# Weighted sums, row buffers and first lists in a hybrid decoder block with gathered experts

## The chip, the cores and the metric

The kernel runs on one core of one Trainium2 chip. The metric is the device time of one execution in microseconds; the time of a kernel is the median of several runs. The profile is one further execution, taken by the hardware profiler. Engines are named PE (TensorE matmul), PEld (TensorE weight load), DVE (VectorE), ACT (ScalarE), POOL (GpSimd) and SP (SyncE).

## The reference

A decoder block over 1024 tokens of width 1024, float32: three token mixers on one normalised input, gated and summed, and then a PEER mixer, in which each token picks 8 x 16 of 16384 experts. The diff is about the second half:

```python
def peer_ffn(h, w_q, subkeys, u, v):
    q = (hf @ w_q).reshape(T, PEER_HEADS, 2, PEER_HALF)
    sc = jnp.einsum('thpd,hpkd->thpk', q, subkeys)
    s1, i1 = lax.top_k(sc[:, :, 0], PEER_TOPK)
    s2, i2 = lax.top_k(sc[:, :, 1], PEER_TOPK)
    cand = (s1[..., :, None] + s2[..., None, :])      # 256 pairs a head
    top_s, pos = lax.top_k(cand, PEER_TOPK)
    ...
    gate = jax.nn.softmax(top_s, axis=-1)
    act = gelu(einsum('chkd,cd->chk', u[ic], hc))     # u rows of the picked experts
    w = gc * act
    return einsum('chk,chkd->cd', w, v[ic])           # weighted sum of their v rows
```

The mixers before it are stick-breaking attention (8 heads), a dilated window attention (12 heads in 3 groups) and cross-attention to 256 memory tokens, each with its own projection, `gates * y` summed, one output projection and the residual.

## The kernel before, in words

The 1024 tokens are 8 tiles of 128, in four groups of two (tiles 0 and 1, 2 and 3, 4 and 5, 6 and 7). `phase1` is a generator that takes one group through projections, the three mixers, gating, output projection, norm (`ffn_norm`), query products (`select`) and, as a side generator, the choice of experts (`topk`). `topk` of a tile makes 16 lists of 16 (`top16`, five VectorE calls each, for 8 heads x 2 halves) into `s16` and `i16`, combines them per head, and ends with the indices `iT` and gates `gT`.

The experts are then computed in one of two ways. Tiles 1, 3 and 5 (`DENSE`) go through all 16384 experts by plain matmul: `dense`, the last stage, streams both expert tables in 64 chunks. The other five tiles gather: 128 steps a tile (class `Experts`), in each of which one u row and one v row of 1024 are fetched per partition with an indirect DMA on POOL. A row here is such a pair of fetches for 128 partitions. In `step`, VectorE multiplies the u row with the token's own h (spread over partitions by a small matmul into `pb`) and sums it (L1037). Every fourth step closes a group of four rows, and a list `behind` runs its later parts one step at a time: `gelu`, then `weights` (the gates times the activations, spread to a 128 x 32 block `wz` per row), then `sums(0)` to `sums(3)`. A `sums` is four matmuls of 32 output columns over the v row, accumulated in `po` (L1061). `supply` fetches u rows ahead; v rows are fetched by `run_behind`, one step after their own.

The h used by the gathered tiles is written to DRAM by `ffn_norm` as three bf16 parts (`part`, L767 to L770, the write on ScalarE's queue) and read back per 32 tokens by `rows_of` into `b3`.

The order of the work: a loop at the end alternates `ex.step()` with `fill`, which advances `phase1` or `dense` by one step and then `nside` steps of the side list (one while rows are there, four while none are). Constants (`TOKEN_NS`, `BW`, `LEAST`) decide how much filling goes between two rows. A scheduler then orders the instructions of each engine from this source order and their readiness, and places waits; ScalarE alone keeps the order of the source.

Group 0 splits its weights and inputs into two float32r halves; the halves live in the row buffers (`spare`), since no rows are gathered yet. A weight is split two ahead of its use.

Of the kernel before, what the change touches and what calls it, by code (L numbers as in the profile page):

```python
# [39 lines left out]
LEAST = 3000.0  # L40
SPLIT = (0,)
AHEAD = 2
UP = 3
GMAX = max(GROUPS)
NMAX = GMAX * 128
QB = 8
# [27 lines left out]
def block_kernel(ctx: ExitStack, tc: tile.TileContext, io):  # L74
    nc = tc.nc
    pool = lambda name, bufs, **kw: ctx.enter_context(tc.tile_pool(name=name, bufs=bufs, **kw))
    gat = pool("gat", 3)
    gw = pool("gw", 2)
    sc = pool("sc", 2)
    keep = pool("keep", 4)  # L80
# [194 lines left out]
        nc.vector.tensor_sub(lo, src, hi)  # L275
        return hi, lo

    nspare = [0]

    def spare():  # L280

        nspare[0] += 1
        t = gat.tile([128, 2, D], F32, name="u" if nspare[0] % 2 else "v").bitcast(F32R)
        return t[:, 0], t[:, 1]

    class Weights:
        def __init__(self, gidx):
# [445 lines left out]
    def ffn_norm(x2, n0, G, h2T):  # L733
        gffn = wp.tile([128, 8, 128], F32, name="w").rearrange("p a b -> p (a b)")
        load(gffn, bass.AP(tensor=io["g_ffn"].tensor, offset=io["g_ffn"].offset,
                                        ap=[[0, 128], [1, D]]))
        h2s = []
        for i in range(G):
            h2 = big.tile([128, D], F32, name="big")
            st = small.tile([128, 4], F32, name="st")  # L740
            actf(h2, x2[:, i, :], AF.Square, accum_out=st[:, 0:1])
            actf(st[:, 1:2], st[:, 0:1], AF.Ln, scale=1.0 / D, bias=eps)
            actf(st[:, 1:2], st[:, 1:2], AF.Exp, scale=-0.5)
            actf(st[:, 2:3], st[:, 1:2], AF.Square)
            nc.vector.tensor_scalar(st[:, 3:4], st[:, 0:1], 1.0 / D, EPS, op0=OP.mult, op1=OP.add)
            nc.vector.scalar_tensor_tensor(st[:, 3:4], st[:, 2:3], -0.5, st[:, 3:4], op0=OP.mult, op1=OP.mult)
            nc.vector.scalar_tensor_tensor(st[:, 1:2], st[:, 3:4], 1.5, st[:, 1:2], op0=OP.add, op1=OP.mult)
            nc.vector.scalar_tensor_tensor(h2, x2[:, i, :], st[:, 1:2], gffn, op0=OP.mult, op1=OP.mult)
            nc.scalar.dma_start(xres[n0 + i], x2[:, i, :])
            h2s.append(h2)  # L750
            cost[0] += 1500
            yield
        for i, h2 in enumerate(h2s):
            for k in range(0, 8, 4):
                pt = bank()
                for j in range(4):
                    flip(pt[:, j * 128:(j + 1) * 128], h2[:, (k + j) * 128:(k + j + 1) * 128])
                actf(h2T[:, k:k + 4, i * 128:(i + 1) * 128], pt.rearrange("p (a b) -> p a b", a=4), AF.Copy)
            yield
        for i, h2 in enumerate(h2s):  # L760
            n = n0 + i
            if n in DENSE:
                nc.scalar.dma_start(h2d[DENSE.index(n)], h2T[:, :, i * 128:(i + 1) * 128])

            for part in range(3 if n not in DENSE else 0):
                b = gw.tile([128, D], BF, name="part", bufs=2)
                nc.vector.tensor_copy(b, h2)  # L767
                if part < 2:
                    nc.vector.tensor_sub(h2, h2, b)
                nc.scalar.dma_start(b3d[n, :, part], b)  # L770
                cost[0] += 1000
                yield
# [8 lines left out]
    def select(pipe, weights, h2T, n0, G, out):  # L781
        N = G * 128
        subk = big.tile([128, 16, 128], F32, name="big")
        load(subk, io["subk"])
        scs = [sc.tile([128, 16, 128], F32, name="sc") for i in range(G)]
        for hp in range(16):
            p = proj_T(weights("w_pq", hp), h2T, N)
            q = tmp.tile([128, NMAX], F32, name="q")
            actf(q[:, :N], p[:, :N], AF.Copy)

            def part(hp=hp, q=q):
                z = bank()
                for i in range(G):
                    mm(z[:, i * 128:(i + 1) * 128], q[:, i * 128:(i + 1) * 128], subk[:, hp, :],
                       start=True, stop=True)
                for i in range(G):
                    actf(scs[i][:, hp, :], z[:, i * 128:(i + 1) * 128], AF.Copy)
            pipe.tick()
            pipe.push(part)
            yield  # L800
        pipe.flush()
        side.append(topk(n0, G, scs, out))

    def topk(n0, G, scs, out):
        for i in range(G):
            s16 = tk.tile([128, 8, 2, 16], F32, name="s16")
            i16 = tk.tile([128, 8, 2, 16], U32, name="i16")  # L810
            for hp in range(16):
                top16(s16[:, hp // 2, hp % 2, :], i16[:, hp // 2, hp % 2, :], scs[i][:, hp, :])
                yield

            room = scs[i].rearrange("p a b -> p (a b)")
            cand = room[:, 0:896].rearrange("p (h c) -> p h c", h=8)
# [83 lines left out]
    def phase1(gidx, n0, G, out):  # L900
        N = G * 128
        pipe = Pipe()
        weights = Weights(gidx)
        xT = big.tile([128, 8, NMAX], F32, name="big")
        load(xT[:, :, :N], io["xT"][:, :, n0 * 128:n0 * 128 + N])
        hT = big.tile([128, 8, NMAX], F32, name="big")
        norm = norm_T(xT, N, g_mix, hT)
        if gidx == 0:
            memT = big.tile([128, 8, MEM], F32, name="big")
            load(memT, io["memT"])  # L910
            mh = big.tile([128, 8, MEM], F32, name="big")
            yield from norm_T(memT, MEM, g_mem, mh)
            kv = memory_kv(pipe, weights, both(gidx, mh, MEM))
            next(kv)
            next(norm)
            yield next(kv)
            next(norm)
            yield next(kv)
            hT = both(gidx, hT, N)
            yield from kv  # L920
            weights.ahead = AHEAD
            gap_tables()
        else:
            yield from norm
            hT = both(gidx, hT, N)
        oT = act.tile([128, 10, NMAX], F32, name="oT")
        yield from stick_breaking(pipe, weights, hT, n0, G, oT)
        mem = memory_attn(pipe, weights, hT, n0, G, oT)
        yield from dilated(pipe, weights, hT, n0, G, oT, mem)
        yield from mem  # L930
        mT = big.tile([128, 8, NMAX], F32, name="big")
        pipe.flush()
        yield from gating(pipe, weights, hT, N, oT, mT)
        x2 = big.tile([128, GMAX, D], F32, name="big")
        yield from out_proj(weights, mT, n0, G, x2)
        h2T = big.tile([128, 8, NMAX], F32, name="big")
        yield from ffn_norm(x2, n0, G, h2T)
        yield from select(pipe, weights, both(gidx, h2T, N), n0, G, out)


    def rows_of(n, c):
        b3 = gw.tile([96, D], BF, name="b3")
        nc.sync.dma_start(b3, b3d[n, c].rearrange("s t d -> (s t) d"))
        return b3

# [4 lines left out]
    class Experts:  # L950
# [5 lines left out]
        def __init__(self):  # L956
            self.tile = None
            self.us, self.vs = [], []
            self.todo = []
            self.behind = []  # L960
            self.late = []

        def fetch(self, kind, ap):

            q = self.us if kind == "u" else self.vs
            if kind not in self.__dict__ or self.__dict__[kind] is None:
                pair = gat.tile([128, 2, D], F32, name=kind)
                x = 0
                self.__dict__[kind] = pair
            else:  # L970
                pair, x = self.__dict__[kind], 1
                self.__dict__[kind] = None
            nc.gpsimd.indirect_dma_start(out=pair[:, x], out_offset=None, in_=io[kind],  # L973
                                         in_offset=bass.IndirectOffsetOnAxis(ap=ap, axis=0))
            q.append(pair[:, x])

        def supply(self):

            while len(self.us) < 2 * UP:
                if self.tile is None:  # L980
                    if not ready:
                        break
# [17 lines left out]
        def run_behind(self):  # L1000

            for it in list(self.behind):
                f = it.pop(0)
                if f:
                    f()
                if not it:
                    self.behind.remove(it)
            if self.late:
                self.fetch("v", self.late.pop(0))

        def step(self):

# [17 lines left out]
                    self.pbs.append(pb)  # L1030
                self.parts = gw.tile([128, 2, 4], F32, name="parts")
            self.run_behind()
            self.late.append(ap)
            u = self.us.pop(0)
            for hh, pb in enumerate(self.pbs):
                f = slice(hh * 512, (hh + 1) * 512)
# [2 lines left out]
            if i == 3:  # L1039
# [13 lines left out]
                def sums(i, wz=wz, box=box):  # L1053
# [10 lines left out]
                    if jj == QB - 1 and i == 3:  # L1064
                        row = box["row"]
                        nc.vector.tensor_add(row, row, po[:, h:h + 256])
                        for k, dst in enumerate(quarters(io["out"][n], c)):
                            nc.scalar.dma_start(dst, row[32 * k:32 * k + 32])
                first = lambda: (weights(), sums(0))
                self.behind.append([gelu, first] + [lambda x=x: sums(x) for x in (1, 2, 3)])  # L1070
            return g == 31 and i == 3

        def flush(self):
# [241 lines left out]
```

## Time and profile before

| | |
|---|---|
| median of 3 runs | 3846.92 us (3844.34 to 3854.73) |
| profiled execution | 3849.53 us |
| its span | 3847.7 us |
| mean granted TensorE clock | 0.964 |
| DMA moved | 1126.05 MB, mean 293 GB/s |
| PE busy | 3582.9 us (93%) |
| DVE busy | 2645.4 us (69%) |
| POOL busy | 1271.1 us (33%), 1280 of its instructions are the fetches |

How to read it: the span runs from the first to the last instruction. Shares of busy time are means over stages. Group 0 takes the first 517 us or so, without rows; groups 1 to 3 with rows beside them go to about 2480 us, the dense stage with the rows of tiles 6 and 7 from there to the end. The chain of waits is followed back from the last instruction; its shares say what set the end. Ends of matmuls are modelled, so matmul times are best read from start to start.

### The profile page before, as it was taken

Reading aid. Unit: us, or ns where it says so; the run is one execution under the profiler, and the core shown is the slowest. Engines: PE = TensorE matmul, PEld = TensorE weight load, DVE = VectorE, ACT = ScalarE, POOL = GpSimd, SP = SyncE. Lnnn points to the kernel's source line nnn. Section 1 sums busy time; section 2 is a strip of 40 time slices with the busy share of each in tenths; the row PEclk is TensorE's granted clock in tenths of the full one; section 3 lists DMA queues with packets and bytes.
Section 4 is the critical chain, followed back from the end, with each engine's and each line's share of the span. In section 5 each row is a group of like instructions: output and inputs, shape, how many; then the busy total and the mean of one; then the engine's idle time right before and its main releaser. Section 6 shows DMA issues by size and latency. Waiting matters only on the chain.

```text
span 3847.7 us, 63068 instructions
## 1 busy us (share of the span) xinstructions
PE 3582.9 (93%) x23493; PEld 2767.8 (72%) x23493; DVE 2645.4 (69%) x7899; ACT 1292.1 (34%) x2584; POOL 1271.1 (33%) x1288
## 2 busy tenths in 40 slices
PE   7999789899799999988999998689999999999999
PEld 6889766677576667767666677576777777777777
DVE  5443697555669656566965665498877877778776
ACT  3442443421225442123554312132322322222322
POOL 0000044333315434320553441024444444434442
PEclk9999899999899999989999999889999999999999
DMA  4435579799969989985998897478999999999995
GB/s 135 135 113 169 179 294 356 282 329 370 342 206 372 364 280 329 358 326 178 358 346 310 318 350 272 149 274 305 340 329 340 340 345 335 338 326 335 354 325 201
DMA packets 365950, 1126.05 MB, mean 293 GB/s; under 512 B 37196, under 2 KB 116812, under 8 KB 344908
## 3 DMA queue, kind: packets, MB, share of 16 engines
q0 software_dynamic: 184320, 671.17, 47.4%
q1 hardware_dynamic: 155024, 403.29, 30.0%
q10 hardware_dynamic: 26300, 47.55, 3.3%
q8 instruction: 186, 3.05, 0.3%
q14 instruction: 120, 0.98, 0.1%
HBM read 1072.78 MB, written 49.09 MB: 292 GB/s over the span
## 4 chain that ended last, share of the span: by engine, by line
PE 78%; DVE 11%; DMA 6%; ACT 2%; issue 1%; ACTq 0%; POOL 0%; SPq 0%; DVEq 0%; POOLq 0%
PE bank L112 36%; PE bank L1080 31%; PE po L1061 9%; DVE u L1037 2%; DMA w<-in_w_gate 2%; PE pb L1028 1%; DMA u<-in_u,iT 1%; DMA b3d<-part 1%; PE bank L116 1%; ACT e L123 1%; DVE ab L1099 1%; DVE sc L777 0%; DVE acc L1197 0%; DVE ab L1101 0%; DMA v<-in_v,iT 0%
## 5 line engine op out<-in xcount | busy, mean ns | idle before, releaser
L973 POOL DMA_INDIRECT u<-in_u,iT x640 | 641.9, 1003 | 1366.2 <-DVE i L776 508.8
L973 POOL DMA_INDIRECT v<-in_v,iT x640 | 628.3, 982 | 1169.9 <-PE po L1061 1041.2
L1037 DVE SCALAR_TENSOR_TENSOR u<-u,pb 128x512 f32<-128x512 f32 x1280 | 835.6, 681 | 69.5 <-DMA u<-in_u,iT 50.2
L112 PE MATMUL bank<-big,w 128*128 128x256 f32 x3072 | 725.1, 390 | 25.2 <-DMA w<-in_w_gate 13.7
L112 PEld LDWEIGHTS bank<-big,w 128*128 128x128 f32 x3072 | 581.5, 194 | 152.9 <-issue 49.0
L1061 PE MATMUL po<-v,wz 128*32 128x256 f32 x5120 | 425.9, 395 | 10.2 <-DVE wz L1050 9.2
L1080 PE MATMUL bank<-hh,uh 128*128 128x384 f32 x1024 | 350.2, 342 | 16.4 <-DVE pos L779 16.2
L1080 PE MATMUL bank<-hh,ul 128*128 128x384 f32 x1024 | 346.7, 339 | 5.2 <-DVE ul L1152 5.2
L1080 PE MATMUL bank<-hl,uh 128*128 128x384 f32 x1024 | 346.0, 338 | 0.0
L1197 DVE TENSOR_TENSOR acc<-acc,bank 128x512 f32<-128x512 f32 x384 | 258.7, 685 | 109.7 <-PE bank L1080 104.4
L1080 PE MATMUL bank<-vh,wh 128*128 128x512 f32 x768 | 324.1, 425 | 3.3 <-ACT wh L123 1.8
L1080 PE MATMUL bank<-vl,wh 128*128 128x512 f32 x768 | 300.2, 394 | 0.0
L1080 PE MATMUL bank<-vh,wl 128*128 128x512 f32 x768 | 298.6, 395 | 0.0
L112 PEld LDWEIGHTS bank<-w,big 128*128 128x128 f32 x2432 | 278.5, 192 | 21.7 <-issue 11.9
L112 PE MATMUL bank<-w,big 128*128 128x128 f32 x2432 | 288.8, 277 | 0.0
L123 ACT ACTIVATE big<-bank 128x128 f32<-128x128 f32 (+2 forms) x436 | 141.6, 419 | 404.2 <-PE bank L112 371.1
L123 ACT ACTIVATE vh<-vr 128x1024 fp32r<-128x1024 f32 x128 | 134.6, 1051 | 411.4 <-PE bank L1080 405.6
L1061 PEld LDWEIGHTS po<-v,wz 128*32 128x32 f32 x5120 | 116.6, 109 | 208.2 <-issue 136.4
L1080 PEld LDWEIGHTS bank<-vh,wh 128*128 128x128 f32 x768 | 143.8, 188 | 117.8 <-issue 70.0
L1080 PEld LDWEIGHTS bank<-hh,uh 128*128 128x128 f32 x1024 | 194.8, 190 | 32.9 <-issue 28.3
L1099 DVE TENSOR_SCALAR ab<-iota,sl 128x128 f32<-128x128 f32 x384 | 134.3, 350 | 104.7 <-PE bank L112 96.6
L1080 PEld LDWEIGHTS bank<-hh,ul 128*128 128x128 f32 x1024 | 195.0, 190 | 11.0 <-DVE ul L1152 9.0
(221 smaller groups left out, 5556.9 us busy)
## 6 DMA issues: line engine op xcount, KB each, us to landing
w<-in_w_in SPq DMA_DIRECT2D x136, 512.0 KB
ur<-in_uT SPq DMA_DIRECT2D x64, 1024.0 KB
vr<-in_vd SPq DMA_DIRECT2D x64, 1024.0 KB
w<-in_w_gate SPq DMA_DIRECT2D x96, 512.0 KB
w<-in_w_pq SPq DMA_DIRECT2D x64, 512.0 KB
gd<-big ACTq DMA_DIRECT2D x24, 1024.0 KB
g<-gd SPq DMA_DIRECT2D x32, 768.0 KB
w<-in_w_o SPq DMA_DIRECT2D x64, 256.0 KB
```

Of the source, the lines that this page charges most:

```text
L112: nc.tensor.matmul(out, lhsT, rhs, **kw)
L116: nc.tensor.transpose(out, in_, ident)
L123: nc.scalar.activation(out, in_, f, **kw)
L973: nc.gpsimd.indirect_dma_start(out=pair[:, x], out_offset=None, in_=io[kind], in_offset=bass.IndirectOffsetOnAxis(ap=ap, axis=0))
L1028: nc.tensor.matmul(pb, which[:, jj].rearrange("p q s -> p (q s)"), box["b3"][:, hh * 512:(hh + 1) * 512], start=True, stop=True)
L1037: nc.vector.scalar_tensor_tensor(u[:, f], u[:, f], 1.0, pb, op0=OP.mult, op1=OP.mult, accum_out=self.parts[:, hh, i:i + 1])
L1061: nc.tensor.matmul(po[32 * k:32 * k + 32, h:h + 256], wz[:, i, :], v[:, 256 * k:256 * k + 256], start=jj == 0 and i == 0, stop=jj == QB - ...
L1080: nc.tensor.matmul(out, lhsT, rhs, **kw)
L1099: nc.vector.tensor_scalar(ab[:, 0, :], iota, sl[:, 0, t:t + 1], sl[:, 2, t:t + 1], op0=OP.is_equal, op1=OP.mult)
L1197: nc.vector.tensor_add(acc[:, i, f], acc[:, i, f], o)
```

## The change

- The four sums of a group are issued together, one step after its weights, instead of one in each of four steps, the first with the weights.
- Rows have buffers of their own: five of u and seven of v, in place of three pairs each. u is fetched up to five ahead, v in the row's own step. `spare` takes one u and one v buffer.
- `part` and `b3` share one pool of three buffers (before: two each).
- `s16` and `i16` get a second buffer; the lists of a group's first tile are made inside `select`, one step behind the scores of each head half, and `topk` makes lists for the other tile alone.
- Group 0 does one more step of the memory projection before it splits hT.

```diff
-UP = 3
+UP, VP = 5, 7
...
-    gat = pool("gat", 3)
+    gat = pool("gat", 1)
...
+    def row_buffer(kind):
+        return gat.tile([128, D], F32, name=kind, bufs=UP if kind == "u" else VP)
     def spare():
-        nspare[0] += 1
-        t = gat.tile([128, 2, D], F32, name="u" if nspare[0] % 2 else "v").bitcast(F32R)
-        return t[:, 0], t[:, 1]
+        return row_buffer("u").bitcast(F32R), row_buffer("v").bitcast(F32R)
...
-                b = gw.tile([128, D], BF, name="part", bufs=2)
+                b = gw.tile([128, D], BF, name="b3", bufs=3)
...
+        s16 = tk.tile([128, 8, 2, 16], F32, name="s16", bufs=2)
+        i16 = tk.tile([128, 8, 2, 16], U32, name="i16", bufs=2)
...
+            def first(hp=hp):
+                top16(s16[:, hp // 2, hp % 2, :], i16[:, hp // 2, hp % 2, :], scs[0][:, hp, :])
             pipe.tick()
-            pipe.push(part)
+            pipe.push(part, first)
...
-            s16 = tk.tile([128, 8, 2, 16], F32, name="s16")
-            i16 = tk.tile([128, 8, 2, 16], U32, name="i16")
-            for hp in range(16):
-                top16(s16[:, hp // 2, hp % 2, :], i16[:, hp // 2, hp % 2, :], scs[i][:, hp, :])
-                yield
+            if i:
+                s16 = tk.tile([128, 8, 2, 16], F32, name="s16", bufs=2)
+                i16 = tk.tile([128, 8, 2, 16], U32, name="i16", bufs=2)
+                for hp in range(16):
+                    top16(s16[:, hp // 2, hp % 2, :], i16[:, hp // 2, hp % 2, :], scs[i][:, hp, :])
+                    yield
...
             yield next(kv)
+            yield next(kv)
             hT = both(gidx, hT, N)
...
-        b3 = gw.tile([96, D], BF, name="b3")
+        b3 = gw.tile([128, D], BF, name="b3", bufs=3)[:96]
...
-            while len(self.us) < 2 * UP:
+            while len(self.us) < UP:
...
-            if self.late:
-                self.fetch("v", self.late.pop(0))
...
-            self.late.append(ap)
+            self.fetch("v", ap)
...
-                first = lambda: (weights(), sums(0))
-                self.behind.append([gelu, first] + [lambda x=x: sums(x) for x in (1, 2, 3)])
+                self.behind.append([gelu, weights, lambda: [sums(x) for x in range(4)]])
```

More of the change, by code (lines that the diff above doesn't have):

```diff
@@ L276, in halves @@
         return hi, lo
-    nspare = [0]
+    def row_buffer(kind):
+        return gat.tile([128, D], F32, name=kind, bufs=UP if kind == "u" else VP)
     def spare():
-        nspare[0] += 1
-        t = gat.tile([128, 2, D], F32, name="u" if nspare[0] % 2 else "v").bitcast(F32R)
-        return t[:, 0], t[:, 1]
+        return row_buffer("u").bitcast(F32R), row_buffer("v").bitcast(F32R)
     class Weights:
@@ L797, in part, with topk @@
                     actf(scs[i][:, hp, :], z[:, i * 128:(i + 1) * 128], AF.Copy)
+            def first(hp=hp):
+                top16(s16[:, hp // 2, hp % 2, :], i16[:, hp // 2, hp % 2, :], scs[0][:, hp, :])
             pipe.tick()
-            pipe.push(part)
+            pipe.push(part, first)
             yield
         pipe.flush()
-        side.append(topk(n0, G, scs, out))
-    def topk(n0, G, scs, out):
+        side.append(topk(n0, G, scs, out, s16, i16))
+    def topk(n0, G, scs, out, s16, i16):
         for i in range(G):
-            s16 = tk.tile([128, 8, 2, 16], F32, name="s16")
-            i16 = tk.tile([128, 8, 2, 16], U32, name="i16")
-            for hp in range(16):
-                top16(s16[:, hp // 2, hp % 2, :], i16[:, hp // 2, hp % 2, :], scs[i][:, hp, :])
-                yield
+            if i:
[4 more added lines that the diff above has]
+                    yield
             room = scs[i].rearrange("p a b -> p (a b)")
@@ L960, in __init__ @@
             self.behind = []
-            self.late = []
         def fetch(self, kind, ap):
[L965 to L973, printed above, removed]
+            t = row_buffer(kind)
+            nc.gpsimd.indirect_dma_start(out=t, out_offset=None, in_=io[kind],
                                          in_offset=bass.IndirectOffsetOnAxis(ap=ap, axis=0))
-            q.append(pair[:, x])
+            (self.us if kind == "u" else self.vs).append(t)
         def supply(self):
-            while len(self.us) < 2 * UP:
+            while len(self.us) < UP:
                 if self.tile is None:
```

## The prediction

> **What bounds the kernel now.** I read the page's totals and its chain first, then the chain by stage, then busy times by stage.
>
> ```profile
> span 3847.7 us, 63068 instructions
> PE 3582.9 (93%) x23493; PEld 2767.8 (72%) x23493; DVE 2645.4 (69%) x7899; ACT 1292.1 (34%) x2584; POOL 1271.1 (33%) x1288
> PE 78%; DVE 11%; DMA 6%; ACT 2%; issue 1%; ACTq 0%; POOL 0%; SPq 0%; DVEq 0%; POOLq 0%
> ...
> by line: PE bank L112 59.8%; PE po L1061 10.2%; DVE u L1037 3.1%; DMA w<-in_w_gate 2.8%; DMA v<-in_v,iT 2.1%; PE bank L116 2.0%; issue 1.8%; DMA u<-in_u,iT 1.7%; PE pb L1028 1.2%; DVE ab L1099 1.2%; DMA b3d<-part 1.2%; DVE ab L1101 1.0%; DV
> by line: PE bank L1080 79.9%; PE po L1061 11.5%; PE pb L1028 2.0%; DMA u<-in_u,iT 1.8%; issue 1.1%; DVE u L1037 0.7%; POOL u L973 0.5%; DVE ul L1152 0.4%; DVE vl L1152 0.3%; DVE acc L1197 0.3%; ACTq L1068 0.2%; POOL v L973 0.2%; DVE w L1179
> ...
> 517.00:2480.00 1963.00, 1817.53 (x12377) 1353.15 (x12376) 1274.06 (x4648) 689.15 (x1579) 728.29 (x762) 0.96 0.86 313
> 2640.00:3848.00 1208.00, 1201.97 (x6992) 910.74 (x6991) 947.45 (x1963) 351.61 (x527) 494.00 (x474) 1.00 0.90 327
> ```
>
> The two "by line" rows are the chain from 1060 to 1740 us (a token group with the gathered rows beside it) and from 2640 to 3848 us (dense experts beside the rows). The window rows have length, then busy time of PE, PEld, DVE, ACT, POOL, then granted clock, DMA share, GB/s. TensorE is the bound: in the dense stage it is busy 1202 of 1208 us and holds 79.9 + 11.5 + 2.0 = 93% of the chain; in a group 59.8 + 10.2 + 2.0 + 1.2 = 73%. The weighted sums (po) alone are a tenth of the chain, so what they cost TensorE is what to price first.
>
> **One: four sums in one go.** A row's sum is four 32-column matmuls, eight records.
>
> ```profile
> L1061 PE MATMUL po<-v,wz x5120: 379/379/637, 526.1 to 3819.6; 128*32 128x256 f32 x197
> ...
> 2909.11 0.40 PE L1080 MATMUL bank<-vh,wl 128*128 128x512 f32 x1
> 2909.43 0.64 PE L1061 MATMUL po<-v,wz 128*32 128x256 f32 x8
> 2910.00 0.50 PE L1080 MATMUL bank<-vh,wh 128*128 128x512 f32 x1
> 2910.34 0.39 PE L1080 MATMUL bank<-vl,wh 128*128 128x512 f32 x1
> 2910.57 0.40 PE L1080 MATMUL bank<-vh,wl 128*128 128x512 f32 x1
> ...
> 3817.75 0.40 PE L1080 MATMUL bank<-vh,wl 128*128 128x512 f32 x1
> 3818.08 1.93 PE L1061 MATMUL po<-v,wz 128*32 128x256 f32 x32
> 3819.94 0.50 PE L1080 MATMUL bank<-vh,wl 128*128 128x512 f32 x1
> 3820.28 0.39 PE L1080 MATMUL bank<-vh,wh 128*128 128x512 f32 x1
> ```
>
> Undisturbed, 512-column matmuls start 0.23 us apart (2910.34 to 2910.57). A row alone costs 2910.34 - 2909.11 = 1.23 us less two such steps, 0.77. Four rows that happen to stand together (the flush at the end) cost 3820.28 - 3817.75 = 2.53 less 0.46, 2.07, where four alone cost 3.08. So each run of sums that is joined to its neighbour saves 1.01/3 = 0.335 us: 0.14 within the run, the rest at its borders, where the next matmuls start late. Counted in the timeline of TensorE from the first sum (526.1) to the last (3819.4), the 640 rows stand in about 560 runs: some 488 alone, 66 pairs, 4 threes, 2 fours. The source after the change makes 160 runs of four. 400 borders x 0.335 = 134 us of TensorE's time.
>
> Of the 1280 POOL fetches 474, 37%, fall into 2640 to 3848 us; with the dense stage's start I take 40% of the rows: 54 us, times the 93% that TensorE has of the chain, 50 us. The groups' 60%, 80 us, times 73% would be 59; right after each group's query products DVE is the fuller engine and in the gating stage weights are waited for (the w_gate entry, 2.8%), so I take 45, with 25 to 59 as ends. Sum: **-95 us**. The weights wz are made one step before the sums rather than in the same step, which takes away this wait of TensorE; I take 5 of it:
>
> ```profile
> PE po L1061 <- DVE wz L1050: 9.2, 8, 2.2
> POOL v L973 <- PE po L1061: 1041.2, 233, 37.2
> DVE u L1037 <- DMA u<-in_u,iT: 50.2, 37, 5.6
> u<-in_u,iT POOLq DMA_INDIRECT x640, 8.2
> ```
>
> **Two: single row buffers.** As many fetches, as many bytes, the same POOL work. The v fetch goes out in the row's own step, ahead of the next u fetch, instead of one step later. A v row of the last place in its group is asked for when the sums four steps before it have freed a buffer and is used four steps on, as now; the other three have more. POOL's 1041 us of waiting for po change shape, and POOL has nothing else to do, so that gains nothing. u is the risk: six rows in three pairs become five. Pace in the dense stage is 1208 us for 474/2 rows, 5.1 us a row, so five rows are 25.5 us ahead of use; a fetch lands after 8.2 us (last column of its row), and a wait for v ahead of it takes 1041.2/233 = 4.5. 12.8 us are left, so the mean fetch stays hidden; the late ones (50.2 us of DVE's waits now) get more by one row's time. I charge **+8**, ends 0 and 25 (half of today's 50 again).
>
> The spare halves in group 0 fall from six to five pairs. Five are enough when two hold h and three hold weights; the split of a weight is then freed by the projection before it, whose copy ScalarE waits for in its queue anyway. **+2**, ends 0 and 8. The added step before hT is split has the remaining memory projections as cover.
>
> **Three: one pool for part and b3.** Today the third bf16 part waits until the first has been written out, and ScalarE's queue, which issues that write, holds the query products behind it.
>
> ```profile
> 404.95 1.23 DVE L769 TENSOR_TENSOR big<-big,part 128x1024 f32<-128x1024 f32 x1
> 414.71 0.69 DVE L767 CAST part<-big 128x1024 bf16<-128x1024 f32 x1 [8.54 <-DMA b3d<-part]
> 418.08 0.80 PE L1080 MATMUL bank<-u 128*128 128x256 f32 x2 [12.94 <-ACT u L123]
> 1723.05 0.71 PE L112 MATMUL bank<-big,q 128*128 128x128 f32 x4 [2.03 <-ACT q L123]
> 2422.55 1.44 PE L1028 MATMUL pb<-b,which 96*128 96x512 bf16 x3 [12.29 <-DMA b<-b3d]
> 400.00:440.00 40.00, 25.77 (x185) 24.73 (x186) 21.94 (x50) 15.12 (x31) 0.00 (x0) 0.73 0.61 200
> ```
>
> With three buffers and no rows running (group 0), the third cast follows at 406.2, so 8.5 of the 12.9 us go. Group 2's last b3 is about done: 2. Group 1 still has a row tile in a buffer: 0. Group 3 makes six parts and then reads b3 into the same three buffers: the cast may come 6 us sooner, or the read 4 us later: 0. Together **-11**, ends -3 and -15. The clock in this window is 0.73; a hole of 4.4 us stays, and no row prices the clock for a hole that short, so I count nothing for it. [...]
>
> **Four: lists during the query products.** The source moves 16 calls of top16 (8 VectorE records each, no DMA) for each group's first tile. But the instruction order on VectorE is not the source's: the lists of the first tile stand among the query products already.
>
> ```profile
> 2435.03 0.29 DVE L775 MAX8 s<-sc 128x8 f32<-128x128 f32 x1 [2.09 <-ACT sc L123]
> 2436.56 0.28 DVE L779 FIND_INDEX8 i<-s,sc 128x8 uint32<-128x128 f32 x1
> 2438.93 0.29 DVE L775 MAX8 s<-sc 128x8 f32<-128x128 f32 x1 [2.09 <-ACT sc L123]
> 2420.00:2480.00 60.00, 57.45 (x279) 50.36 (x279) 24.07 (x113) 11.88 (x43) 0.00 (x0) 0.93 0.34 109
> 2500.00:2620.00 120.00, 96.79 (x544) 79.41 (x544) 117.35 (x374) 34.70 (x47) 36.03 (x32) 0.87 0.76 267
> ```
>
> One list takes 2435.03 to 2436.84 = 1.8 us and then waits 2.09 for the next scores. So the move itself is worth 0. What does change is that s16 and i16 get a second buffer: today the second tile's lists start only when the first tile has let go of them, in 2500 to 2620 us, where DVE is busy 117 of 120 us and TensorE misses 23. If they slip into the 2.09 us gaps, up to 16 x 1.8 = 29 us of DVE leave that stretch. I take half, **-15**, ends 0 (they stay) and -30. In group 0 the weight splits fill those gaps; nothing there.
>
> **Sum.** -95 - 5 + 8 + 2 - 11 - 15 = -116. The profiled execution took 3849.5 us (span 3847.7), 2.6 over the median of the runs shown: 3733 in its terms, **3731** in the median's.
>
> **Rivals.**
> - *The transfers become the bound.* DMA share is already 0.86 to 0.90 in the two long windows. For it: w_gate waits on the chain. Against it: 327 x 1208/1158 = 341 GB/s would do for the dense stage, and this window moved more:
> ```profile
> 1160.00:1220.00 60.00, 59.20 (x360) 39.57 (x360) 54.65 (x220) 31.77 (x50) 36.20 (x37) 1.00 0.99 379
> ```
>  Half of the 95 lost and 10 more of u waits: about 3789.
> - *The sums don't stay together.* Engine orders are not the source's, so a row whose v is thought late may be put behind other matmuls. Then parts two to four remain, -21 to -25: about 3825.
> - *Nothing measurable*: that, with part four worth nothing and u waits at their end: 3840 to 3855.
> - *Slower: the gather queue.* A v fetch at the head of POOL's queue now waits for a whole burst of sums, all u fetches behind it, with one u row less in store; a late u delays parts, wz, and TensorE's burst with all behind it. It decides once the 12.8 us reserve is gone and more than 116/160 = 0.73 us a group is lost; at 1 us a group 160 - 116 = +44, about 3893. The row of 1041 us speaks for it, the reserve against. [...]
>
> **How the numbers follow.** Forecast 0.66, transfers 0.14, sums apart 0.07, nothing 0.05, slower 0.08. The forecast's own ends: all the better ones (50 + 59 from the sums, 9 of wz, 15, 30) give about 3684, all the worse ones (50 + 25, nothing of wz, 3, nothing from part four, 33 lost) about 3802. The range 3690 to 3815 takes in the forecast and the transfers; left out are 0.20. Faster by over 0.3% (11.5 us, about what runs of this kernel can tell from nothing): 0.66 + 0.14 + 0.07 = 0.87; within 0.05; slower 0.08.
>
> **What will show it.** Right: po records in blocks of 32, 1.93 us each, about 160 runs; PE busy down by 100 us or more at a span down as much; the hole at 405 us down to some 4 us; lists of the second tile between 2425 and 2482. Wrong: po in eights; DVE's waits for u far over 50 us or TensorE's for v where there are none now; DMA share near 1.0 in the dense windows with TensorE no longer full.

## The result, and the profile after

| | before | after |
|---|---|---|
| median | 3850.77 us (3844.34 to 3854.73) | 3782.09 us (3779.82 to 3798.13) |
| span of the profiled execution | 3847.7 us | 3780.4 us |
| mean granted TensorE clock | 0.964 | 0.957 |
| PE busy | 3582.9 us | 3462.0 us |
| DMA moved | 1126.05 MB | 1126.09 MB |

The ratio is 0.9832, with a 95% interval of 0.98 to 0.9864: 69 us faster, where 116 were forecast. The page after: totals, the chain by engine, and the group of the sums (with that of before above it).

```profile
L1061 PE MATMUL po<-v,wz 128*32 128x256 f32 x5120 | 425.9, 395 | 10.2 <-DVE wz L1050 9.2 <-DMA v<-in_v,iT 0.8
```
```profile
span 3780.4 us, 63673 instructions
PE 3462.0 (92%) x23493; PEld 2829.0 (75%) x23493; DVE 2617.4 (69%) x7899; ACT 1297.7 (34%) x2588; POOL 1265.3 (33%) x1288
...
PE 70%; DVE 11%; DMA 9%; issue 4%; ACT 4%; POOL 2%; ACTq 1%; SPq 0%; POOLq 0%; DVEq 0%
...
L1057 PE MATMUL po<-v,wz 128*32 128x256 f32 x5120 | 336.5, 386 | 17.5 <-DVE wz L1046 17.5
```

TensorE does the same 23493 matmuls in 121 us less, 89 of them in the sums' own records. But the span fell by 67 only, TensorE's share of the chain fell from 78 to 70%, and the granted clock is 0.957 instead of 0.964. TensorE now stands idle for longer than before, 318 us of the span instead of 265. The waits say where:

```profile
POOL u L971 <- DVE u L1033: 807.4, 364, 15.6
POOL v L971 <- PE po L1057: 509.4, 217, 36.0
...
DVE u L1033 <- DMA u<-in_u,iT: 109.5, 66, 5.9
...
PEld bank L112 <- DVE sc L874: 48.8, 4, 13.5
PE bank L112 <- DVE sc L874: 47.3, 4, 13.1
```

The columns are the sum in us, how many waits, and the longest. POOL's two rows are waits for a free row buffer, and POOL has nothing else to do. Two rows that matter are worse than before: VectorE waits 109.5 us for u rows (50.2 before), and TensorE waits 47.3 us in four waits, one per group, for `sc`. The same row of before reads:

```profile
PE bank L112 <- DVE sc L869: 9.3, 4, 5.7
```

`sc` here holds a tile's indices, with which `topk` ends (L874 is the line that writes them). TensorE turns them, and then the gates, by small matmuls of 32 columns each; these are called the turning below. TensorE's timeline at group 1's first tile, before and after:

```profile
1118.28 0.71 PE L112 MATMUL bank<-big,q 128*128 128x128 f32 x4
...
1150.13 0.63 PE L112 MATMUL bank<-S,none 128*128 128x128 f32 x2
1151.69 0.65 PE L112 MATMUL bank<-ident,sc 128*32 128x32 f32 x32 [0.92 <-DVE sc L869]
```
```profile
1112.47 0.71 PE L112 MATMUL bank<-big,q 128*128 128x128 f32 x4
...
1127.26 6.00 PE L112 MATMUL bank<-big,w 128*128 128x256 f32 x16 [8.48 <-DVE big L336]
1145.65 0.65 PE L112 MATMUL bank<-ident,sc 128*32 128x32 f32 x32 [12.39 <-DVE sc L874]
```

Before, TensorE works on the next group's attention (`S`, `sp`) until the indices are there. After, it reaches the turning matmuls when they aren't, and stands 12.39 us in front of them, with that attention queued behind. The others are 13.05 (group 0), 12.03 and 9.85 us. Yet the choice is no earlier: the turning begins about 33 us after the last query product in both kernels (1118.99 to 1151.69 before, 1113.18 to 1145.65 after).

The 8.48 us for `big` in the timeline after are another wait that came with the moved lists: TensorE waits 25.5 us for `big` in groups 1 to 3, and 11.5 before. The fastest kernels below (`lag` and its like) have these 25.5 us too, so they are not what set the change back; what they cost was not tried.

By stages, in us, from landmarks in TensorE's timeline (attention: from the end of the query products to the first matmul of gating with `w_o`; rest: output projection to the end of the query products; sums over groups 1 to 3):

| kernel | attention | gating | rest | group 0 | dense |
|---|---|---|---|---|---|
| before | 1050.2 | 502.2 | 456.2 | 473.7 | 1365.4 |
| after | 1094.4 | 480.9 | 431.5 | 472.8 | 1300.9 |
| joined sums alone (`burst`) | 1070.1 | 481.9 | 450.8 | 475.8 | 1314.0 |
| turning put back (`lag`) | 1046.2 | 482.4 | 443.5 | 468.8 | 1299.7 |
| the same, sums apart (`lag_apart`) | 1049.6 | 505.5 | 450.5 | 468.1 | 1350.1 |
| one list buffer (`list1`) | 1048.6 | 483.8 | 443.6 | 471.5 | 1313.6 |
| the same, two pools (`list1_parts`) | 1050.2 | 484.7 | 450.9 | 472.1 | 1313.7 |

The dense stage and gating gained; attention, with three of the four waits, lost 44 us. The last five rows are experiments.

### The profile page after: what moved, and what is told of

It reads as the page before. It is cut to its first block, busy times and chain, and to the rows that moved or that the text cites. A ratio compares the mean times of both kernels' runs of the same rounds, so it can differ in the third digit from the quotient of the medians.

```text
span 3780.4 us, 63673 instructions
## 1 busy us (share of the span) xinstructions
PE 3462.0 (92%) x23493; PEld 2829.0 (75%) x23493; DVE 2617.4 (69%) x7899; ACT 1297.7 (34%) x2588; POOL 1265.3 (33%) x1288
## 2 busy tenths in 40 slices
DMA packets 365955, 1126.09 MB, mean 298 GB/s; under 512 B 37196, under 2 KB 116812, under 8 KB 344908
## 4 chain that ended last, share of the span: by engine, by line
PE 70%; DVE 11%; DMA 9%; issue 4%; ACT 4%; POOL 2%; ACTq 1%; SPq 0%; POOLq 0%; DVEq 0%
PE bank L112 33%; PE bank L1075 28%; PE po L1057 7%; DMA u<-in_u,iT 4%; DMA w<-in_w_gate 2%; PE pb L1024 1%; DVE u L1033 1%; PE bank L116 1%; POOL u L971 1%; DVE ul L1147 1%; POOL v L971 1%; DVE w L1174 1%; DVE vl L1147 1%; DMA v<-in_v,iT 1%; ACT wh L123 1%
## 5 line engine op out<-in xcount | busy, mean ns | idle before, releaser
L971 POOL DMA_INDIRECT u<-in_u,iT x640 | 631.7, 987 | 1817.5 <-DVE u L1033 807.4
L1033 DVE SCALAR_TENSOR_TENSOR u<-u,pb 128x512 f32<-128x512 f32 x1280 | 835.9, 680 | 143.0 <-DMA u<-in_u,iT 109.5
L971 POOL DMA_INDIRECT v<-in_v,iT x640 | 632.7, 989 | 657.3 <-PE po L1057 509.4
L112 PE MATMUL bank<-big,w 128*128 128x256 f32 x3072 | 722.3, 390 | 43.6 <-DVE big L336 25.5
L1057 PE MATMUL po<-v,wz 128*32 128x256 f32 x5120 | 336.5, 386 | 17.5 <-DVE wz L1046 17.5
L1057 PEld LDWEIGHTS po<-v,wz 128*32 128x32 f32 x5120 | 155.3, 110 | 158.1 <-issue 39.6
```

The costliest lines, as they stand in the source:

```text
L112: nc.tensor.matmul(out, lhsT, rhs, **kw)
L971: nc.gpsimd.indirect_dma_start(out=t, out_offset=None, in_=io[kind], in_offset=bass.IndirectOffsetOnAxis(ap=ap, axis=0))
L1033: nc.vector.scalar_tensor_tensor(u[:, f], u[:, f], 1.0, pb, op0=OP.mult, op1=OP.mult, accum_out=self.parts[:, hh, i:i + 1])
L1057: nc.tensor.matmul(po[32 * k:32 * k + 32, h:h + 256], wz[:, i, :], v[:, 256 * k:256 * k + 256], start=jj == 0 and i == 0, stop=jj == QB - ...
```

## The experiments

Three theories stood for the missing 47 us. **T**: the transfers set the pace in the groups, so time saved on TensorE is waited for at rows and weights. **W**: part four costs something, since without the lists' 16 side steps the turning matmuls stand earlier in TensorE's queue. **C**: the rows come from an earlier point, since a tile is handed on 16 side steps sooner, and crowd the attention stage. The first expectations were written before W; they call C theory L, and have a fourth, **S**: five u buffers are too few. Kernels that were run together share the median of before: 3846.98 for the first four, 3849.75 for the next four, 3845.93 for the last.

**The changed kernel again** (`again`).

> The changed kernel once more, on the same chip as the others of this set, so that they have something to be compared with. All theories: about 3782 us, 65 to 70 below the kernel before.

3783.67 us, ratio 0.9835 (0.9814 to 0.9857). The loss against the forecast is no accident of one run.

**Joined sums alone on the kernel before** (`burst`).

```diff
-                first = lambda: (weights(), sums(0))
-                self.behind.append([gelu, first] + [lambda x=x: sums(x) for x in (1, 2, 3)])
+                self.behind.append([gelu, weights, lambda: [sums(x) for x in range(4)]])
```

> The kernel before with part one alone: four sums in one go, row buffers in three pairs each and the lists as before. Measured so far: the dense stage gained 64 us, the group stages nothing, though TensorE has 121 us less to do. Theory T (in the groups the gathered rows' transfers set the pace, TensorE's saving shows in the dense stage alone): about 55 us faster than before, 3795, all of it in the dense stage. Theory S (five u buffers are too few in the groups and take back what the sums bring there): the groups gain too, 95 us faster, 3755. Theory L (the first tile's lists, moved ahead in the source, make rows start earlier and crowd the attention stages): as S, 3755.

3787.94 us, ratio 0.9845 (0.9825 to 0.9864): 59 us gained, 51 of them in the dense stage (1365.4 to 1314.0); in the groups gating gained 20 and attention lost 20. This is what T had said, and neither S nor L. Part one alone gives nearly all that the whole change gives, so the rest of it nets to almost nothing.

**Six buffers each** (`u6v6`).

```diff
-UP, VP = 5, 7
+UP, VP = 6, 6
```

> The changed kernel with six u and six v buffers in place of five and seven. T: as the changed kernel within 10 us (3772 to 3792), waits of VectorE for u fall, but the time doesn't. S: waits of VectorE for u from 110 us back to some 50 and 35 us or more faster, 3745. L: as the changed kernel.

3773.89 us, ratio 0.9814 (0.9795 to 0.9834): 10 us under `again`, though the intervals overlap. S had 35 us or more, and is not borne out. VectorE's waits for u fall, to the row below, and TensorE's for `sc` stay (46.7 us):

```profile
DVE u L1033 <- DMA u<-in_u,iT: 82.7, 59, 5.4
```

**First lists back in the side steps** (`lists`), the two buffers of `s16` and `i16` kept.

```diff
-            pipe.push(part, first)
+            pipe.push(part)
...
-            if i:
-                s16 = tk.tile([128, 8, 2, 16], F32, name="s16", bufs=2)
-                i16 = tk.tile([128, 8, 2, 16], U32, name="i16", bufs=2)
+            if True:
+                if i:
+                    s16 = tk.tile([128, 8, 2, 16], F32, name="s16", bufs=2)
+                    i16 = tk.tile([128, 8, 2, 16], U32, name="i16", bufs=2)
```

> The changed kernel with the first tile's lists back in the side generator (s16 and i16 keep their two buffers). T: rows start later in the source, the attention stages lose some 15 rows and get 30 to 45 us shorter, the stages after them as much longer: the total within 10 us of the changed kernel. S: no change in the total, nor in the waits for u. L: 40 us faster than the changed kernel, 3742.

3749.28 us, ratio 0.9749 (0.973 to 0.9768), 34 us under `again` on the same chip. Moving these lists in the source was the loss. TensorE's waits for `sc` fall to 14.2 us:

```profile
PE bank L112 <- DVE sc L875: 14.2, 4, 5.7
```

T had expected the total to stay within 10 us. This doesn't yet part W from C: the move took 16 side steps from ahead of both the turning and the rows. The next two part them, on the changed kernel: the first puts the turning 16 side steps later, and with it the rows, which `topk` hands on behind it; the second puts only the rows there.

**The turning, and the rows behind it, put back** (`lag`): `LAG` is the number of side steps between the end of the choice and the turning matmuls, 1.

```diff
-            for _ in range(LAG):
+            for _ in range(LAG if i else LAG + 16):
```

> The changed kernel, with the first tile's lists still inside the query products, but the small matmuls that turn its indices (sc and s against the identity) placed 16 side steps later, where they stood in the source before. Measured so far: with the lists back in the side generator the time was 3749, and TensorE's wait for sc at these matmuls, 47.3 us in four waits, was gone. Theory W (TensorE stands in its queue at these matmuls, because the source brings them 16 steps earlier while VectorE needs the same time as before): that wait is near 0 and the time 3749 (3740 to 3760). Theory C (the rows start earlier and crowd the attention stages, whatever TensorE waits for): rows start as late as before here too, so also 3749; it tells these two from a third, that the lists inside the query products cost VectorE's or ScalarE's time there: then 3782.

3743.03 us, ratio 0.9723 (0.9707 to 0.9739). The lists are made where the change puts them; the turning and what follows it in `topk` stand 16 side steps later in the source, and some 39 us come back. TensorE's waits and the same place in its timeline:

```profile
PE bank L112 <- DVE sc L874: 2.0, 1, 2.0
```
```profile
1104.39 0.71 PE L112 MATMUL bank<-big,q 128*128 128x128 f32 x4
...
1137.71 1.22 PE L112 MATMUL bank<-sp,ntri 128*128 128x256 f32 x2 [0.48 <-DVE sp L451]
1138.86 0.66 PE L112 MATMUL bank<-ident,sc 128*32 128x32 f32 x32
```

The turning now stands behind attention's work and waits for nothing, and it comes as long after the query products as ever: 33.8 us (1105.10 to 1138.86), though 16 side steps later in the source. The granted clock is lower around the wait, too. These are the 57 us from group 1's last query products on, in the kernel after and in `lag`; both have the wait for `big`, and `lag` lacks the other:

```profile
1113.00:1170.00 57.00, 32.47 (x229) 23.41 (x227) 53.57 (x238) 16.54 (x33) 16.21 (x18) 0.76 0.56 201
```
```profile
1105.00:1162.00 57.00, 44.28 (x288) 32.29 (x287) 54.25 (x214) 25.82 (x46) 16.44 (x17) 0.88 0.61 212
```

The columns are those of the prediction's window rows. In `lag` TensorE is busy for 44.28 us instead of 32.47, at a granted clock of 0.88 instead of 0.76. This kernel is called the mended one below.

**The rows alone put back** (`late_rows`).

```diff
+            if i == 0:
+                for _ in range(16):
+                    yield
             out.append((n0 + i, iT, gT))
```

> The changed kernel, with the turning matmuls early in the source as they are there, but the tile given to the row loop 16 side steps later. W: TensorE still waits some 47 us for sc, the time stays near 3782. C: rows in the attention stages go back from 260 to some 243 and the time to 3749.

3791.14 us, ratio 0.9846 (0.9828 to 0.9863): no gain. The rows that VectorE works on during attention fall, by group, from 76, 88 and 96.5 to 69.5, 85.5 and 89.5, about as many as in `lag` (69, 85.5, 89.5), but TensorE's wait stays:

```profile
PE bank L112 <- DVE sc L874: 47.2, 4, 12.9
```

W holds and C has fallen: the rows alone bring nothing. This kernel and `lag` have the rows equally late and differ in where the turning stands, and that makes 48 us (3791.14 to 3743.03); attention alone differs by 54 (1099.9 to 1046.2), more than the three waits in it last.

**One buffer for the lists** (`list1`): `lists` with `s16` and `i16` allocated in `topk` with `bufs=1`, as before the change.

> The changed kernel with the lists back in the side generator and one buffer each of s16 and i16, as before the change. The prediction gave the second buffer 15 us (0 to 30): then 3764, VectorE in the stretch after the last query products as full as before and TensorE's idle there back to some 40 us. If the second buffer does nothing: 3749.

3757.97 us, ratio 0.976 (0.9743 to 0.9776), 9 us over `lists` by the medians, 4 by the ratios, with overlapping intervals. The trace shows the mechanism more plainly. Windows of `lists` and then of `list1`, in which group 3's query products end at 2451 and 2447; then VectorE's list calls of `list1` from 2500 to 2540:

```profile
2480.00:2520.00 40.00, 33.10 (x235) 26.97 (x234) 37.74 (x92) 12.59 (x17) 15.90 (x16) 0.91 0.78 273
2520.00:2560.00 40.00, 39.30 (x241) 32.49 (x240) 39.70 (x121) 14.96 (x21) 14.40 (x14) 1.00 0.92 326
```
```profile
2480.00:2520.00 40.00, 32.70 (x236) 27.18 (x237) 38.91 (x134) 11.40 (x16) 16.85 (x16) 0.96 0.81 287
2520.00:2560.00 40.00, 33.41 (x169) 27.18 (x168) 39.31 (x164) 11.07 (x16) 9.89 (x9) 0.91 0.79 268
```
```profile
L777 DVE MAX8 s<-sc 128x8 f32<-128x128 f32 x12 | 3.4, 283 | 0.0
L774 DVE MAX8 s<-sc 128x8 f32<-128x128 f32 x11 | 3.0, 282 | 0.0
```

With one buffer, 11 to 12 of the second tile's 16 lists still lie there; with two there are none left, and TensorE is busy 39.3 of 40 us instead of 33.4 in the next window.

**Half the bytes of each row** (`half`): `lists`, but each fetch brings only the first 512 of a row's 1024 columns, which the products and the sums read twice, so all engines do the same work. It leaves the second half of the expert rows out.

```diff
-            nc.gpsimd.indirect_dma_start(out=t, out_offset=None, in_=io[kind],
+            nc.gpsimd.indirect_dma_start(out=t[:, :512], out_offset=None, in_=io[kind + "2"],
...
```

> The changed kernel with the lists back in the side generator, and fetches of the first 512 columns of each u and v row alone (2 KB in place of 4 KB a partition); VectorE and TensorE use these columns twice, so their work is as before and the second half of each row's part is left out. Theory T (in groups 1 to 3 the rows' transfers set the pace): these groups, 1983 us with whole rows, get 100 us shorter or more, down to what TensorE needs. Rival (TensorE and the chains between engines set it there too): 30 us or less. In the dense stage, where TensorE is full, both expect 30 us or less.

3747.06 us in one run, against 3749.28 of `lists`. Page rows and one dense window of `half`, then the window of `lists`:

```profile
DMA packets 284035, 790.54 MB, mean 211 GB/s; under 512 B 37196, under 2 KB 116812, under 8 KB 262988
...
q0 software_dynamic: 102400, 335.63, 28.6%
...
2640.00:3700.00 1060.00, 1057.72 (x6433) 867.32 (x6432) 873.24 (x1828) 327.42 (x488) 470.19 (x447) 1.00 0.72 240
```
```profile
2640.00:3700.00 1060.00, 1057.71 (x6431) 866.75 (x6430) 870.44 (x1824) 326.91 (x488) 468.29 (x449) 1.00 0.96 353
```

30% fewer bytes, a DMA share of 0.72 instead of 0.96, and TensorE does the same 6430 matmuls in the same time. T has fallen, in the dense stage and over the whole, as far as one run can show it: groups 1 to 3 together got 8 us shorter, where T had 100 or more. Gating did get faster (482.5 to 463.9), but attention (1055.6 to 1062.1), rest (444.9 to 449.4) and dense (1297.4 to 1304.2) gave it back.

**Sums apart in the mended kernel** (`lag_apart`): `lag`, with the sums as before the change, one in each step.

> The kernel with the late turning matmuls (3743 us), but with the four sums one step after another again, the first with its weights; everything else as there. It prices part one where the other parts are in place. By the prediction's terms (50 in the dense stage, 45 in the groups, 5 of wz) it would be 100 slower, 3843. If the saving shows in the dense stage alone, as between the kernel before and the one with part one alone (dense 51 us, groups 5): about 55 slower, 3798.

3827.16 us, ratio 0.9955 (0.9942 to 0.9968). Joining is worth 84 us here by the medians (3827.16 to 3743.03) and 89 by the ratios, against 59 on the kernel before; of the two expectations, 100 and 55, neither is met. By stages: dense 50.4, gating 23, rest 7, attention 3. The same dense window of `lag` and then of `lag_apart`:

```profile
2640.00:3700.00 1060.00, 1057.69 (x6450) 865.68 (x6450) 871.77 (x1827) 326.71 (x488) 465.93 (x447) 1.00 0.95 351
```
```profile
2640.00:3700.00 1060.00, 1059.43 (x6160) 800.51 (x6161) 839.88 (x1751) 310.42 (x465) 445.76 (x430) 1.00 0.92 339
```

TensorE is full in both, and does 290 matmuls more in the same 1060 us when the sums are joined: here, where it is the bound, what the borders cost came off the time, 50.4 us in the dense stage.

**One pool undone** (`list1_parts`): `list1`, with `part` and `b3` in pools of two again. Against `burst` it has the single row buffers, the v fetch in the row's own step and the added memory step.

> The changed kernel with lists in the side generator, one s16 and i16 buffer (3758 us), and two buffers each for part and b3, as before the change. The prediction gave the shared pool 11 us: then 3769, with the hole before group 0's query products back to 12.9 us. What then still lies between this kernel and the one with part one alone (3788) is due to the single row buffers and the earlier v fetch: the prediction had charged them 8 to 10 us, here they would be worth some 19 of gain.

3771.44 us, ratio 0.9808 (0.9782 to 0.9834). So the shared pool is worth 13.5 us by the medians (3771.44 to 3757.97) and 18 by the ratios. The buffers are worth some 16 us against `burst` (14 by the ratios); the two intervals overlap a little. Group 0's hole, in `list1_parts` and in the kernel after:

```profile
415.64 0.58 PE L1073 MATMUL bank<-u 128*128 128x256 f32 x1 [13.83 <-ACT u L123]
```
```profile
416.41 0.58 PE L1075 MATMUL bank<-u 128*128 128x256 f32 x1 [8.40 <-ACT u L123]
...
400.00:440.00 40.00, 27.43 (x192) 26.40 (x193) 26.55 (x86) 18.38 (x38) 0.00 (x0) 0.74 0.68 225
```

In the kernel after, the third cast no longer waits, but the next write that ScalarE's queue issues takes 4.29 us, where the kernel before needs 0.59:

```profile
409.08 0.69 DVE L766 CAST b<-big 128x1024 bf16<-128x1024 f32 x1
...
410.97 4.29 ACTq L762 DMA_DIRECT2D h2d<-big  x1
415.30 1.06 ACT L123 ACTIVATE u<-big 128x1024 fp32r<-128x1024 f32 x1 [6.66 <-issue]
```

**The mended kernel with six and six** (`lag_u6v6`).

> The kernel with the late turning matmuls and six u and six v buffers. In the changed kernel six and six were worth 10 us (3784 to 3774). If that is the u store, and not chance in the order of instructions, it is worth about 10 here too: 3733, VectorE's wait for u below 74 us. If the store is large enough as it is: 3743.

3739.59 us, ratio 0.973 (0.9706 to 0.9754), 3 us under `lag` by the medians and not told apart from it. VectorE's waits for u are 59.1 us, against 73.9 in `lag`. These two are the best versions, 39 to 43 us under the changed kernel.

**More filling between rows on top of it** (`lag_u6v6_tok`): the price of a row in the loop at the end, which lowered lets more filling go between two rows.

```diff
-TOKEN_NS, TOKEN_BYTES = 700.0, 128 * 8192 + 3 * 8192.0
+TOKEN_NS, TOKEN_BYTES = 500.0, 128 * 8192 + 3 * 8192.0
```

> As the kernel with late turning matmuls and six and six buffers, with the row's TensorE price in the row loop (TOKEN_NS) at 500 ns in place of 700, since four joined sums cost 0.52 us a row where they cost 0.77 alone: more filling goes between two rows, and rows reach further into the stages after the attention. If TensorE's stalls in the attention stages come from rows standing too close there, 10 to 20 us faster than with 700; if not, the same within 10 us.

3779.04 us, ratio 0.9822 (0.9804 to 0.9839): 39 us slower, where 10 to 20 faster or the same was expected. Attention has fewer rows (65.5, 76.5 and 85.5 by group) and is faster (1027.9 against 1044.0), but the stage rest takes 488.9 instead of 442.7 and the dense stage 1321.1 instead of 1299.3. Rows left over from one stage are paid for in another.

## Why the prediction was right or wrong, point by point

The direction was right, the size not: 69 us of 116. By the runs, the parts add up thus (differences of medians, some over two sets of runs): sums alone -59, row buffers -16, pool -13.5, second list buffer -9, moved lists +34. That is -64, where -63 to -69 was measured; the runs form a chain from the one kernel to the other, so such a sum has to agree but for noise. Order matters, as the sums show: 59 us on the kernel before, 84 on the mended one. Taken in this order, the sums and wz gave 41 us less than their 100, the moved lists cost 34 that the forecast had at 0, and the row buffers and spare halves, charged with 10, gave 16. These 26 us that nobody had priced made up for part of the two losses; that the forecast is off by no more than 47 us is partly luck.

- **The step that failed: "So the move itself is worth 0."** That VectorE makes the first tile's lists among the query products in either kernel was read correctly, and it was taken for the whole effect. But the 16 calls were also 16 side steps between the end of `select` and the turning matmuls. VectorE's lists went where the scheduler had them already; TensorE's turning went up by 16 steps in its queue, and while four side steps go with each step of filling, that is four steps of attention which used to stand ahead of it. The choice was no earlier, and TensorE stood 47.3 us in front of it, where 9.3 had been. The cost is 34 us by `lists`, 39 by `lag` and 48 between `late_rows` and `lag`: beside the sums in the groups, the largest error of the prediction. The prediction counted every instruction that moved, and none that stayed in the source while its neighbours left.
- **Joined sums, -95, and wz, -5.** The price was about right: 121 us of PE busy went, of 134 expected. Part of the rest is that the sums stand in about 190 runs and not 160: a count in the timeline that bridges breaks of up to three other matmuls gives 563 runs before and 187 after, 134 of them whole bursts of 32 records. By that count 376 borders went, 0.32 us each; with every break counted it is 609 and 208, and 0.30 us each. A whole run in the dense stage, after:

```profile
2928.75 0.39 PE L1075 MATMUL bank<-vh,wl 128*128 128x512 f32 x1
2929.07 1.93 PE L1057 MATMUL po<-v,wz 128*32 128x256 f32 x32
2930.93 0.50 PE L1075 MATMUL bank<-vh,wh 128*128 128x512 f32 x1
```

  The 1.93 us are as read from the flush. What TensorE does at a border no run shows; what one costs is 0.30 to 0.32 us by these counts. Dense was said to give 50 and gave 51 (`burst`) and 50.4 (`lag_apart`). The groups' 45, ends 25 and 59, came to 33 in the mended kernel and, on the kernel before, to some 5 (the stage table: 20 and 5 gained, 20 lost). That the waits for wz would fall was wrong: 9.2 before, 17.5 after.
- **u store, +8, and spare halves, +2.** Wrong in sign. The waits for u did rise, from 50.2 to 109.5 us, to far over 50 as the prediction's list of wrong signs has it. But the buffers as a whole gained: `list1_parts` has 20 us less attention than `burst` (1050.2 to 1070.1) although its waits for u are longer (71.8 against 64.5). A likely reason is that in pairs a burst of four holds four of six v rows until its sums are done; this was argued and not tried alone, nor were the spare halves and the added memory step. Six u and six v buffers instead of five and seven gave 10 us on the changed kernel and 3 on the mended one, both with overlapping intervals, so that share is not shown.
- **One pool, -11 (ends -3 and -15).** 13.5 measured, so the size was right, in part by luck, for its place was only half right. "8.5 of the 12.9 us go" came to 4.5, with 8.40 left: the cast's wait went whole, but 3.7 us of it came back as the longer issue of `h2d`. Of the gain between `list1_parts` and `list1` the stage table has 7.3 us in the stage rest of groups 1 to 3 (450.9 to 443.6), which were priced at 2, and 0.6 net in group 0 (472.1 to 471.5). No gain was counted for the clock, and none came: with the hole a third shorter (8.40 us instead of 12.94) the window from 400 to 440 us has 0.74, against 0.73. How the clock goes with the length of a hole isn't shown by that, for it is down before this hole begins: 0.50 already from 398 to 405 us in the kernel before and from 402 to 408.5 in the kernel after, where in either a shorter hole, of 5.6 us, ends.
- **Second buffer of the lists, -15 (ends 0 and -30).** 9 by the medians, 4 by the ratios, so its size is not settled, but the mechanism is the one described: 29 lists instead of 15 fall into 2425 to 2482, before and after:

```profile
L775 DVE MAX8 s<-sc 128x8 f32<-128x128 f32 x15 | 4.4, 295 | 33.9 <-ACT sc L123 33.9
```
```profile
L774 DVE MAX8 s<-sc 128x8 f32<-128x128 f32 x29 | 7.1, 285 | 22.0 <-ACT sc L123 22.0
```

- **Rivals.** The nearest in time, 3789 with the transfers as the bound, was the wrong reason, as `half` shows: the DMA share near 1.0 (0.96 in the dense window of `lists`) went with a full TensorE, busy 1057.71 of 1060 us. The sums stayed together. That u fetches stand behind a waiting v fetch is so in the trace of the kernel before: POOL waits 10.21 us in front of the v fetch at 937.99 us, and the u fetches at 940.48 and 941.72 come after it with no wait of their own. POOL's wait for sums fell from 1041.2 to 509.4 us and its wait for free u buffers rose from 305.1 to 807.4; with late u rows at 73.9 us in `lag`, against 50.2 before, the gather queue didn't turn it.

## What to carry to other kernels

When a source step is taken out, look at what came after it as well as at the step itself: an engine whose order follows the source gets the later instructions sooner, and may stand in front of one whose data is no earlier, as TensorE did here (47.3 us in four waits). Putting the turning 16 side steps later in the source (`lag`) brought 39 us. Small matmuls of another tile shape (here 128x32 among 128x128) were cheaper issued in runs, by 0.30 to 0.32 us a border, and a high DMA share (0.96) was no sign of a bound: with half the bytes of each row it fell to 0.72, and TensorE did as many matmuls in the same time (one run).

## What the runs showed of the hardware

TensorE didn't pass a matmul that waited: it stood 9.9 to 13.1 us four times, three times with attention work queued and the fourth with the dense stage's, and the granted clock of the 57 us around one of these waits was 0.76; in `lag`, which lacks the wait, it was 0.88. TensorE's weight loader stood just as long (48.8 us in four waits). Fetching 2 KB instead of 4 KB per partition took 30% of all bytes away and changed the time by 2 us of 3749 (one run).
